# Global attention of a diffusion layer: the context scores join the latent scores' row, with one maximum and one exponential a head

## The chip, the cores and the metric

The kernel runs on one core of a Trainium2 chip. The time is device microseconds of one execution, and the median of three executions is compared. One further execution was profiled, and its trace is what the views below read. PE is the matrix engine, PEld its weight loads, DVE the vector engine, ACT the scalar engine, POOL the general engine, SP the queue from which most transfers are issued. Every engine takes its instructions in the order of its own queue.

## What is computed

A layer over 1024 latent tokens and 256 context tokens of width 1024: two attention branches side by side, gated and merged, a layer norm, and a gated feed-forward part with a short convolution. All of it is float32. The change touches the second branch, global attention with 8 heads of 64 in two groups of four, whose keys are the 1024 latent and the 256 context ones in one softmax:

```python
def _global_attention(q, k_all, v_all):
    bsz, n_tok = q.shape[:2]
    def one_block(i):
        q_blk = lax.dynamic_slice_in_dim(q, i * BLOCK, BLOCK, axis=1)
        p = jax.nn.softmax(_gqa_scores(q_blk, k_all), axis=-1)
        return _gqa_values(p, v_all)
...
    o_b = _global_attention(q_b, jnp.concatenate([k_b, k_b_c], axis=1), jnp.concatenate([v_b, v_b_c], axis=1))
```

## The kernel before

A float32 product is made of float32r ("rounded") parts: an operand is split into a high part, which is a cast, and a low part, which is what the cast left, and two or three matmuls are added up.

Attention works through 32 **units**, one for each branch, block of 128 queries and group of four heads: 16 units of the windowed branch 0, then 16 of the global branch 1, in the order (block, group). A unit of branch 1 is named 1_i_g. It has two halves:

- *Scores*, in the loop's turn u of the unit. For each head h, `lat` (L508) multiplies the queries with 1024 latent keys (four matmuls of 512 columns) into a PSUM tile `s` of two banks, of which there are two. One DVE instruction (L538) multiplies the scores by the negative scale into the SBUF tile `p` and reduces them to the head's minimum `nm` (which is minus the maximum); its second scalar is the start value of that reduction. ACT then takes the exponential in place (L505, called through `soft`) and adds up the row (`sm`).
- *Values* (`value_steps`, L601), one turn later, spread between the next unit's score steps. For each of ten blocks n of 128 keys (0 to 7 latent, 8 and 9 context), PE transposes the four heads' pieces of `p` into a PSUM tile `ptr` (L614), ACT casts it to `pth` (L623), DVE takes the rest as `ptl` (L624), and two matmuls with `pth` and `ptl` add to `av` (L635, L636). For blocks 2 and 6 ACT copies the tile out to `prw` (L620), which frees it, and POOL makes both parts.

The context keys of a unit go their own way in branch 1. `cxp` (L541), ahead of the four heads, writes the scores of all four heads with 256 context keys into a fifth `s` tile. DVE reduces it to four maxima (L550) and scales them (L551, `nmc`); ACT takes four exponentials of 256 (L505, tile `p_x`) relative to the context's maximum. `nmc` is also the start value of the latent reduction, so `nm` is the joint one. `norm` (L558) afterwards works out f = exp(nm − nmc) and POOL multiplies the context's sums and its four pieces of `p_x` by f (L564, L565, L568).

PSUM has eight banks: two `s` tiles of two, three tiles `pt` of one (transposes `ptr`, the query transposes `qtr`, the row of sums `str`, and the output tiles `b` of the first branch's projection, which fills turns 18 to 30), and one for `av`. `p` has eight SBUF tiles of 1024 columns. A unit of branch 1 takes five of them, and a tile comes free with its last transposition.

The order on each queue is not the order of the code: in this stage a list scheduler places the instructions of all turns by its own estimates, and a tile of a pool is handed on when the last reader of its previous content is done. The order it made is shown below where the prediction needs it.

Of the kernel before, what the change touches and what calls it, by code (L numbers as in the profile page):

```python
# [7 lines left out]
F32 = mybir.dt.float32  # L8
R32 = mybir.dt.float32r
AF = mybir.ActivationFunctionType  # L10
# [3 lines left out]
P = 128  # L14
D = 1024
T = 1024
# [11 lines left out]
HALF = 512  # L28
POOL_LO = (3,), (2, 6)
# [39 lines left out]
def layer_kernel(  # L69
# [393 lines left out]
    class Unit:  # L463
# [40 lines left out]
        def soft(self, s, p, h, nm, sm, scale):  # L504
            nc.scalar.activation(p, s, AF.Exp, bias=nm[:, h:h + 1], scale=scale, accum_out=sm[:, h:h + 1])  # L505

        def lat(self, h):
# [29 lines left out]
            p = p_tile(f"p{self.id}_{h}")[:, 0:T if self.br else self.w + NC]  # L537
            nc.vector.tensor_scalar(out=p, in0=o, scalar1=self.qscale(nqs)[:, hs] if self.br else -1.0,  # L538
                                    scalar2=self.other[:, hs], op0=ALU.mult, op1=ALU.min, accum_out=self.nm[:, hs])
            self.soft(p, p, h, self.nm, self.sm, -1.0)  # L540
            self.pc[h, 0] = p  # L541

        def cxp(self):
            kh = self.br * 2 + self.g
            s = s_tile(f"s{self.id}_x")
            for h in range(4):
                self.qk(s[:, h * NC:(h + 1) * NC], h, KC[0][:, kh])
            self.other = small(f"nmc_{self.id}", (P, 4))
            self.smc = small(f"smc_{self.id}", (P, 4))
            nc.vector.reduce_max(self.other, s.rearrange("p (a b) -> p a b", a=4), axis=AX.X)  # L550
            nc.vector.tensor_tensor(out=self.other, in0=self.other, in1=self.qscale(nqs), op=ALU.mult)  # L551
            p = p_tile(f"p{self.id}_x")
            for h in range(4):
                self.pc[h, 1] = p[:, h * NC:(h + 1) * NC]
                self.soft(s[:, h * NC:(h + 1) * NC], self.pc[h, 1], h, self.other, self.smc,
                          self.qscale(pqs)[:, h:h + 1])

        def norm(self):  # L558
            hc = slice(self.g * 4, self.g * 4 + 4)
            f = small(f"f_{self.id}", (P, 4))  # L560
            if self.br:
                nc.vector.tensor_tensor(out=f, in0=self.nm, in1=self.other, op=ALU.subtract)
                nc.scalar.activation(f, f, AF.Exp)
                nc.gpsimd.tensor_tensor(out=self.smc, in0=self.smc, in1=f, op=ALU.mult)  # L564
                nc.gpsimd.tensor_tensor(out=self.sm, in0=self.sm, in1=self.smc, op=ALU.add)  # L565
                for h in range(4):
                    p = self.pc[h, 1]
                    nc.gpsimd.tensor_scalar(out=p, in0=p, scalar1=f[:, h:h + 1], scalar2=0.0, op0=ALU.mult, op1=ALU.add)  # L568
            else:
                nc.vector.tensor_tensor(out=f, in0=self.nm, in1=sinkb[:, hc], op=ALU.add)  # L570
                nc.scalar.activation(f, f, AF.Exp)
                nc.vector.tensor_tensor(out=self.sm, in0=self.sm, in1=f, op=ALU.add)
                nc.vector.reciprocal(self.sm, self.sm)
# [17 lines left out]
        def score_steps(self):  # L591
            steps = [lambda h=h: self.lat(h) for h in range(4)]
            return steps + [self.norm]

        def context(self):
            self.begin()
            if self.br:
                self.cxp()

        def pslice(self, h, n):  # L600
            if self.br and n >= NT:  # L601
                return self.pc[h, 1][:, (n - NT) * P:(n - NT + 1) * P]
            return self.pc[h, 0][:, n * P:(n + 1) * P]
# [300 lines left out]
    def p_tile(name):  # L904
        return att.tile([P, T], F32, tag="p", name=name, bufs=8)
# [1019 lines left out]
```

## Time and profile before

| what | value |
|---|---|
| median of three runs | 1564.17 us (1563.13 to 1565.62) |
| profiled execution, its own time | 1565.22 us |
| span in its trace, first to last instruction | 1563.4 us |
| PE busy | 1531.6 us of the span |
| DVE, ACT, POOL busy | 1187.6, 808.6, 782.2 us |
| scores of branch 1 | from 457.9 us (first context scores) to about 744 us |
| last values of branch 1 | about 756 us |

A row of a timeline gives the start in us from the span's start, the time until the last of its instructions ends, engine, line, operation, tiles (written <- read), shape and count; in brackets stands the idle time of the engine before it and who ended that. Matmuls overlap: a row's time is a latency, and the pace of PE is read from one start to the next. Rows of groups give count, busy time, the mean of one in ns, and the idle time before them by releaser. Rows of waits give who waited for whom, the sum, the number of times and the longest.

### The profile page before, as it was taken

What the parts mean: (1) busy time and instruction counts of PE and PEld (TensorE: products, weight loads), DVE (VectorE), ACT (ScalarE), POOL (GpSimd) and SP (SyncE); (2) the same over time, 40 slices, a digit from 0 to 9 for tenths busy, and PEclk for the clock granted to TensorE, in tenths of its full rate; (3) what the DMA queues carried; (4) which work ended last, traced back from release to release, by engine and by line L of the source; (5) the groups of instructions that cost most, each with busy time, mean ns of one, the idle gap of its engine ahead of it and who ended that gap; (6) DMA issues with size and microseconds to landing.
All of it is one profiled execution on the core that took longest, in us unless ns stands there. A gap on an engine that the chain in (4) does not pass through costs nothing.

```text
span 1563.4 us, 22286 instructions
## 1 busy us (share of the span) xinstructions
PE 1531.6 (98%) x7804; PEld 1282.2 (82%) x7804; DVE 1187.6 (76%) x1714; ACT 808.6 (52%) x1431; POOL 782.2 (50%) x795
## 2 busy tenths in 40 slices
PE   9999999999999999999999999999999999999997
PEld 7888888888877877877888997888888888888887
DVE  6677976548887777777774788888888888657884
ACT  5322223358887777777431673544444444435552
POOL 0356422526666777776332455666677764121121
PEclk9999999999999999999999999999999999999998
DMA  9776662322235666631550223233334446996721
GB/s 371 267 239 239 207 245 92 106 84 66 65 116 137 150 149 151 148 80 35 180 184 16 98 79 120 81 112 115 120 102 114 113 117 191 363 265 212 251 103 55
DMA packets 113105, 232.11 MB, mean 148 GB/s; under 512 B 13056, under 2 KB 27904, under 8 KB 112896
## 3 DMA queue, kind: packets, MB, share of 16 engines
q1 hardware_dynamic: 97760, 201.82, 38.4%
q0 software_dynamic: 10400, 20.19, 8.3%
q10 hardware_dynamic: 4832, 8.68, 1.5%
q8 instruction: 61, 1.00, 0.3%
q14 instruction: 52, 0.43, 0.1%
HBM read 179.45 MB, written 65.86 MB: 157 GB/s over the span
## 4 chain that ended last, share of the span: by engine, by line
PE 54%; DVE 3%; ACT 1%; issue 1%; POOL 0%; DVEq 0%; ACTq 0%
PE p L89 4%; PE p L90 4%; PE p L91 4%; PE b L89 2%; PE b L91 2%; PE b L90 2%; PE c L89 2%; PE c L91 2%; PE d L91 2%; PE d L89 2%; PE c L90 2%; PE d L90 2%; PE a L91 2%; PE a L89 2%; PE a L90 2%; PE y L91 2%
## 5 line engine op out<-in xcount | busy, mean ns | idle before, releaser
L624 DVE TENSOR_TENSOR ptl<-ptr,pth 128x512 fp32r<-128x512 f32 x190 | 126.2, 682 | 32.6 <-ACT pth L623 32.2
L623 ACT CAST pth<-ptr 128x512 fp32r<-128x512 f32 x190 | 108.0, 593 | 54.0 <-PE ptr L614 32.6
L86 DVE TENSOR_TENSOR ld<-rd,hd 128x1024 fp32r<-128x1024 f32 x77 | 94.9, 1249 | 50.2 <-ACT hd L81 48.1
L505 ACT ACTIVATE p<-p,nm 128x1024 f32<-128x1024 f32 (+2 forms) x128 | 125.9, 985 | 4.5 <-DVE p L538 4.3
L614 PE MATMUL ptr<-ident,p 128*128 128x128 f32 x816 | 122.4, 277 | 4.4 <-DVE ptl L624 3.2
L81 ACT CAST hd<-rd 128x1024 fp32r<-128x1024 f32 x77 | 79.5, 1050 | 81.1 <-PE p L91 55.1
L614 PEld LDWEIGHTS ptr<-ident,p 128*128 128x128 f32 x816 | 94.1, 141 | 25.6 <-DVE ptl L624 7.9
L86 POOL TENSOR_TENSOR wlg<-wg,whg 128x512 fp32r<-128x512 f32 x32 | 47.7, 1500 | 123.3 <-ACT whg L81 123.3
L635 PE MATMUL av<-pth,VT 128*128 128x512 f32 x236 | 104.6, 443 | 2.1 <-ACT avs L641 1.5
L89 PE MATMUL p<-hd 128*128 128x512 f32 x264 | 103.2, 391 | 0.0
L91 PE MATMUL p<-hd,ld 128*128 128x512 f32 x264 | 102.7, 389 | 0.0
L90 PE MATMUL p<-ld,hd 128*128 128x512 f32 x264 | 102.7, 389 | 0.0
L636 PE MATMUL av<-ptl,VT 128*128 128x512 f32 x236 | 98.1, 416 | 2.7 <-POOL ptl L86 2.7
L89 PE MATMUL g<-hh,whg 128*128 128x512 f32 x256 | 99.9, 390 | 0.0
L91 PE MATMUL g<-hh,wlg 128*128 128x512 f32 x256 | 99.7, 389 | 0.0
L90 PE MATMUL g<-hl,whg 128*128 128x512 f32 x256 | 99.6, 389 | 0.0
L538 DVE TENSOR_SCALAR_CACHE_REDUCE p<-s,cvt,nmc 128x1024 f32<-128x1024 f32 x64 | 83.2, 1316 | 8.8 <-PE s L494 7.7
L493 PE MATMUL s<-KL,q 128*128 128x512 f32 (+2 forms) x192 | 75.6, 394 | 5.3 <-ACT p_x L505 2.8
L787 ACT ACTIVATE sg<-g,bgc 128x512 f32<-128x512 f32 x32 | 22.0, 686 | 96.1 <-PE g L91 96.1
L494 PE MATMUL s<-KL,q 128*128 128x512 f32 (+2 forms) x192 | 71.6, 373 | 0.0
L81 ACT CAST wS<-s 128x512 fp32r<-128x512 f32 x76 | 45.3, 620 | 46.4 <-POOL s L1227 45.7
L81 ACT CAST wA<-ru 128x512 fp32r<-128x512 f32 x57 | 35.5, 623 | 62.4 <-PE d L91 33.8
(436 smaller groups left out, 5015.2 us busy)
## 6 DMA issues: line engine op xcount, KB each, us to landing
wml<-in_wmodT_dram SPq DMA_DIRECT2D x48, 512.0 KB
ru<-in_w_up_dram SPq DMA_DIRECT2D x38, 512.0 KB
rd<-td SPq DMA_DIRECT2D x55, 256.0 KB
rd<-sd SPq DMA_DIRECT2D x44, 256.0 KB
rd<-in_w_dn_dram SPq DMA_DIRECT2D x33, 256.0 KB
wm<-in_wmodT_dram SPq DMA_DIRECT2D x16, 512.0 KB
wg<-in_w_g_dram SPq DMA_DIRECT2D x32, 256.0 KB
sgd<-sg ACTq DMA_DIRECT2D x32, 256.0 KB
```

Source lines behind the costliest of these rows:

```text
L81: nc.scalar.copy(hi, src)
L86: lo_eng.tensor_tensor(out=lo, in0=src, in1=hi.bitcast(F32), op=ALU.subtract)
L89: nc.tensor.matmul(ps, a[0], b[0], start=start, stop=False, skip_group_check=resumed)
L90: nc.tensor.matmul(ps, a[0], b[1], start=False, stop=False, skip_group_check=resumed)
L91: nc.tensor.matmul(ps, a[1], b[0], start=False, stop=stop, skip_group_check=resumed)
L505: nc.scalar.activation(p, s, AF.Exp, bias=nm[:, h:h + 1], scale=scale, accum_out=sm[:, h:h + 1])
L538: nc.vector.tensor_scalar(out=p, in0=o, scalar1=self.qscale(nqs)[:, hs] if self.br else -1.0, scalar2=self.other[:, hs], op0=ALU.mult, op1 ...
L614: nc.tensor.transpose(tr[:, h * P:(h + 1) * P], self.pslice(h, n), ident)
L623: nc.scalar.copy(hi, tr)
L624: nc.vector.tensor_tensor(out=lo, in0=tr, in1=hi.bitcast(F32), op=ALU.subtract)
L635: nc.tensor.matmul(self.av, v, hi, start=first, stop=False)
L636: nc.tensor.matmul(self.av, v, lo, start=False, stop=self.left == 0)
```

## The change

For branch 1, `p` becomes a row of 1280 columns, 1024 latent and 256 context keys. `cxp(h0)` now serves two heads: it takes a one-bank `pt` tile (`sx`), writes two times 256 context scores, takes the two heads' `p` tiles, and lets DVE scale each head's context scores into columns 1024 to 1279, with their minimum as `nmc` (new line 555; the reduction starts at the constant FBIG). It is called for heads 0 and 1 ahead of the unit's scores and for heads 2 and 3 between `lat(1)` and `lat(2)`. `lat` then writes the other 1024 columns into the same tile, and one exponential of 1280 columns with one row sum follows (new line 544). The fifth `s` tile, the reductions L550 and L551, the four exponentials of 256, `norm` in branch 1 and POOL's four multiplications go. `p` has six tiles of 1280 columns. In the windowed branch two heads share one such tile.

```diff
-            p = p_tile(f"p{self.id}_{h}")[:, 0:T if self.br else self.w + NC]
-            nc.vector.tensor_scalar(out=p, in0=o, scalar1=self.qscale(nqs)[:, hs] if self.br else -1.0,
+            if self.br:
+                p = self.pc[h]
+                row, out = p, p[:, 0:T]
+            else:
+                if h % 2 == 0:
+                    self.pair = p_tile(f"p{self.id}_{h}").rearrange("p (a b) -> p a b", a=2)
+                out = row = self.pair[:, h % 2, 0:self.w + NC]
+            nc.vector.tensor_scalar(out=out, in0=o, scalar1=self.qscale(nqs)[:, hs] if self.br else -1.0,
                                     scalar2=self.other[:, hs], op0=ALU.mult, op1=ALU.min, accum_out=self.nm[:, hs])
-            self.soft(p, p, h, self.nm, self.sm, -1.0)
+            nc.scalar.activation(row, row, AF.Exp, bias=self.nm[:, hs], scale=-1.0, accum_out=self.sm[:, hs])
...
-        def cxp(self):
+        def cxp(self, h0):
             kh = self.br * 2 + self.g
-            s = s_tile(f"s{self.id}_x")
-            for h in range(4):
-                self.qk(s[:, h * NC:(h + 1) * NC], h, KC[0][:, kh])
...
-            nc.vector.reduce_max(self.other, s.rearrange("p (a b) -> p a b", a=4), axis=AX.X)
-            nc.vector.tensor_tensor(out=self.other, in0=self.other, in1=self.qscale(nqs), op=ALU.mult)
-            p = p_tile(f"p{self.id}_x")
-            for h in range(4):
-                self.pc[h, 1] = p[:, h * NC:(h + 1) * NC]
-                self.soft(s[:, h * NC:(h + 1) * NC], self.pc[h, 1], h, self.other, self.smc,
-                          self.qscale(pqs)[:, h:h + 1])
+            s = pt_tile(f"sx{self.id}_{h0}")
+            for n, h in enumerate((h0, h0 + 1)):
+                self.qk(s[:, n * NC:(n + 1) * NC], h, KC[0][:, kh])
+            for n, h in enumerate((h0, h0 + 1)):
+                hs = slice(h, h + 1)
+                self.pc[h] = p = p_tile(f"p{self.id}_{h}")
+                nc.vector.tensor_scalar(out=p[:, T:NK], in0=s[:, n * NC:(n + 1) * NC], scalar1=self.qscale(nqs)[:, hs],
+                                        scalar2=FBIG, op0=ALU.mult, op1=ALU.min, accum_out=self.other[:, hs])
...
-            if self.br:
-                nc.vector.tensor_tensor(out=f, in0=self.nm, in1=self.other, op=ALU.subtract)
-                nc.scalar.activation(f, f, AF.Exp)
-                nc.gpsimd.tensor_tensor(out=self.smc, in0=self.smc, in1=f, op=ALU.mult)
-                nc.gpsimd.tensor_tensor(out=self.sm, in0=self.sm, in1=self.smc, op=ALU.add)
-                for h in range(4):
-                    p = self.pc[h, 1]
-                    nc.gpsimd.tensor_scalar(out=p, in0=p, scalar1=f[:, h:h + 1], scalar2=0.0, op0=ALU.mult, op1=ALU.add)
...
             steps = [lambda h=h: self.lat(h) for h in range(4)]
-            return steps + [self.norm]
+            if not self.br:
+                return steps + [self.norm]
+            steps.insert(2, lambda: self.cxp(2))
+            return steps
...
-        return att.tile([P, T], F32, tag="p", name=name, bufs=8)
+        return att.tile([P, NK], F32, tag="p", name=name, bufs=6)
```

The scheduler places the rest anew. Two places of one turn are shown; the turns of the other units of branch 1 look alike. The names: `p1_3_0_2` is the row of unit 1_3_0, head 2; `ptl1_2_1_7` the low part of block 7 of the unit before it; `bT` a product of the projection that fills in; the brackets give the engines that an instruction waits for.

First DVE's queue in the turn of unit 1_3_0, before the change, from the reciprocal of the previous unit's sums:

```order
L581 RECIPROCAL rb1_2_1_6469<-str1_2_1_6467 4x128 [waits DMAHW2_49,DMAHW7_49,DMAHW1_49,PE_49]
L538 TENSOR_SCALAR p1_3_0_2_6456,nm_1_3_0_6320<-s1_3_0_2_6451,cvt_69,nmc_1_3_0_6331 128x1024 [waits PE_49]
L538 TENSOR_SCALAR p1_3_0_3_6464,nm_1_3_0_6320<-s1_3_0_3_6459,cvt_69,nmc_1_3_0_6331 128x1024 [waits PE_49]
L624 TENSOR_TENSOR ptl1_2_1_7_6501<-ptr1_2_1_7_6495,pth1_2_1_7_6500 128x512 [waits PE_49,Activation_49]
L562 TENSOR_TENSOR f_1_3_0_6475<-nm_1_3_0_6320,nmc_1_3_0_6331 128x4 [waits DVE_49]
L951 TENSOR_TENSOR bT0_5_6510<-b0_5_0_6512,bT0_5_6510 128x512 [waits DMAHW6_49,PE_49]
L624 TENSOR_TENSOR ptl1_2_1_8_6545<-ptr1_2_1_8_6539,pth1_2_1_8_6544 128x512 [waits Activation_49]
L624 TENSOR_TENSOR ptl1_2_1_9_6554<-ptr1_2_1_9_6548,pth1_2_1_9_6553 128x512 [waits PE_49,Activation_49]
```

The same place in DVE's queue after the change:

```order
L572 RECIPROCAL rb1_2_1_6355<-str1_2_1_6353 4x128 [waits DMAHW2_49,DMAHW7_49,DMAHW1_49,PE_49]
L617 TENSOR_TENSOR ptl1_2_1_7_6385<-ptr1_2_1_7_6379,pth1_2_1_7_6384 128x512 [waits PE_49,Activation_49]
L944 TENSOR_TENSOR bT0_5_6394<-b0_5_0_6396,bT0_5_6394 128x512 [waits DMAHW6_49,PE_49]
L555 TENSOR_SCALAR p1_3_0_2_6342,nmc_1_3_0_6218<-sx1_3_0_2_6337,cvt_69 128x256 [waits PE_49]
L555 TENSOR_SCALAR p1_3_0_3_6344,nmc_1_3_0_6218<-sx1_3_0_2_6337,cvt_69 128x256 [waits PE_49]
L542 TENSOR_SCALAR p1_3_0_2_6342,nm_1_3_0_6216<-s1_3_0_2_6346,cvt_69,nmc_1_3_0_6218 128x1024 [waits DVE_49]
L542 TENSOR_SCALAR p1_3_0_3_6344,nm_1_3_0_6216<-s1_3_0_3_6361,cvt_69,nmc_1_3_0_6218 128x1024 [waits DVE_49]
L617 TENSOR_TENSOR ptl1_2_1_8_6429<-ptr1_2_1_8_6423,pth1_2_1_8_6428 128x512 [waits Activation_49]
L617 TENSOR_TENSOR ptl1_2_1_9_6438<-ptr1_2_1_9_6432,pth1_2_1_9_6437 128x512 [waits Activation_49]
```

The two instructions of 1024 columns for heads 2 and 3 moved from ahead of `ptl` 7 to behind it, with two of 256 columns in front of them, each of which waits for PE.

Then PE's queue at the turn from unit 1_3_0 to 1_3_1, before the change, right behind the last transposes of block 9 (`s1_3_1_x` is the tile of context scores, `q11`, `q21` the two query tiles):

```order
L636 MATMUL av1_2_1_6404<-ptl1_2_1_5_6446,VT2_2137 128x512
L493 MATMUL s1_3_1_x_6561<-KC_2134,q11_3_1_6289 128x256
L494 MATMUL s1_3_1_x_6561<-KC_2134,q21_3_1_6290 128x256 [waits DMAHW5_49,DMAHW4_49]
L493 MATMUL s1_3_1_x_6561<-KC_2134,q11_3_1_6289 128x256
L494 MATMUL s1_3_1_x_6561<-KC_2134,q21_3_1_6290 128x256
```

And after it, four `av` matmuls and the two heads' context scores `sx1_3_1_0` behind those transposes:

```order
L494 MATMUL s1_3_1_0_6479<-KL3_2133,q11_3_1_6185 128x512 [waits DVE_49]
L495 MATMUL s1_3_1_0_6479<-KL3_2133,q21_3_1_6186 128x512
L494 MATMUL s1_3_1_0_6479<-KL3_2133,q11_3_1_6185 128x512
L495 MATMUL s1_3_1_0_6479<-KL3_2133,q21_3_1_6186 128x512
L494 MATMUL s1_3_1_1_6527<-KL3_2133,q11_3_1_6185 128x512 [waits DVE_49]
L495 MATMUL s1_3_1_1_6527<-KL3_2133,q21_3_1_6186 128x512
L494 MATMUL s1_3_1_1_6527<-KL3_2133,q11_3_1_6185 128x512
L607 MATMUL ptr1_3_0_0_6455<-ident_58,p1_3_0_0_6224 128x128 [waits DVE_49,PE_49]
L607 MATMUL ptr1_3_0_0_6455<-ident_58,p1_3_0_1_6226 128x128
L607 MATMUL ptr1_3_0_0_6455<-ident_58,p1_3_0_2_6342 128x128 [waits Activation_49]
L629 MATMUL av1_2_1_6291<-ptl1_2_1_8_6429,VT4_2139 128x512
L628 MATMUL av1_2_1_6291<-pth1_2_1_9_6437,VT4_2139 128x512
```

The latent scores of the next unit's heads 0 and 1 moved from behind the first two blocks of transposes to ahead of them, and each now waits for DVE.

A little later in the same queue, after the change:

```order
L607 MATMUL ptr1_3_0_2_6486<-ident_58,p1_3_0_0_6224 128x128 [waits DVE_49]
L607 MATMUL ptr1_3_0_2_6486<-ident_58,p1_3_0_1_6226 128x128
L607 MATMUL ptr1_3_0_2_6486<-ident_58,p1_3_0_2_6342 128x128
L607 MATMUL ptr1_3_0_2_6486<-ident_58,p1_3_0_3_6344 128x128
L495 MATMUL s1_3_1_1_6527<-KL3_2133,q21_3_1_6186 128x512
L607 MATMUL ptr1_3_0_3_6497<-ident_58,p1_3_0_0_6224 128x128 [waits Activation_49]
```

The first transpose of block 3 waits for ACT; before the change it waited for DVE (the same line then read [waits DVE_49]).

More of the change, by code (lines that the diff above doesn't have):

```diff
@@ L28 @@
 HALF = 512
+FBIG = 3.0e38
 POOL_LO = (3,), (2, 6)
@@ L502, in qscale @@
             return t[:, self.i, self.g * 4:self.g * 4 + 4]
-        def soft(self, s, p, h, nm, sm, scale):
-            nc.scalar.activation(p, s, AF.Exp, bias=nm[:, h:h + 1], scale=scale, accum_out=sm[:, h:h + 1])
         def lat(self, h):
@@ L560, in norm @@
             f = small(f"f_{self.id}", (P, 4))
[L561 to L573 removed]
+            nc.vector.tensor_tensor(out=f, in0=self.nm, in1=sinkb[:, hc], op=ALU.add)
+            nc.scalar.activation(f, f, AF.Exp)
+            nc.vector.tensor_tensor(out=self.sm, in0=self.sm, in1=f, op=ALU.add)
+            nc.vector.reciprocal(self.sm, self.sm)
         def rows(self):
@@ L597, in context @@
             if self.br:
-                self.cxp()
+                self.other = small(f"nmc_{self.id}", (P, 4))
+                self.cxp(0)
         def pslice(self, h, n):
-            if self.br and n >= NT:
-                return self.pc[h, 1][:, (n - NT) * P:(n - NT + 1) * P]
-            return self.pc[h, 0][:, n * P:(n + 1) * P]
+            return self.pc[h][:, n * P:(n + 1) * P]
         def value_steps(self):
```

4 lines of the change are left out of this document (1 added, 3 removed).

## Prediction

> **What bounds the kernel now.** I read the page, the busy time by stage, the waits of PE and its weight loads in the stage of the second branch, and then that stage's timelines. The page's span, and the stage in three windows (PE, PEld, DVE, ACT, POOL busy, then the clock):
>
> ```profile
> span 1563.4 us, 22286 instructions
> PE 54%; DVE 3%; ACT 1%; issue 1%; POOL 0%; DVEq 0%; ACTq 0%
> 458.00:500.00 42.00, 36.68 (x203) 28.68 (x204) 32.45 (x55) 33.45 (x79) 27.59 (x43) 0.96 0.60 142
> 500.00:755.00 255.00, 248.65 (x1438) 204.37 (x1438) 194.76 (x297) 186.47 (x401) 190.59 (x275) 1.00 0.48 116
> 755.00:1563.00 808.00, 796.32 (x3851) 671.97 (x3849) 627.16 (x670) 372.55 (x506) 363.37 (x243) 0.99 0.46 144
> ```
>
> PE sets the end, in this stage and behind it: from 500 to 755 us it is idle for only 255 − 248.65 = 6.4 us. ACT (73%), POOL (75%) and DVE (76%) have room. What leaves those three is worth something only where PE waits for it, and 755 to 1563 us is PE work too, so a shift at 755 should reach the end whole. Who kept PE and its weight loads waiting:
>
> ```profile
> PEld av L635 <- ACT avs L641: 5.7, 11, 0.7
> PEld s L493 <- ACT p_x L505: 5.3, 6, 1.0
> PEld av L636 <- POOL ptl L86: 1.0, 2, 0.7
> PEld s L493 <- DVE p L538: 0.5, 1, 0.5
> PEld av L636 <- POOL ptl L86: 2.8, 2, 1.8
> ```
>
> The first four are of 500 to 755 us, the last of 458 to 500. Six times the next scores wait until ACT has read the four context scores out of the `s` tile. What one costs, and PE's pace, is read from start to start:
>
> ```profile
> 671.91 0.60 PE L614 MATMUL ptr<-ident,p_x 128*128 128x128 f32 x4
> 672.27 0.48 PE L636 MATMUL av<-ptl,VT 128*128 128x512 f32 x1
> 672.59 0.28 PE L493 MATMUL s_x<-KC,q 128*128 128x256 f32 x1
> 672.71 0.28 PE L494 MATMUL s_x<-KC,q 128*128 128x256 f32 x1
> ...
> 677.91 0.40 PE L636 MATMUL av<-ptl,VT 128*128 128x512 f32 x1
> 678.90 0.50 PE L493 MATMUL s<-KL,q 128*128 128x512 f32 x1 [0.59 <-ACT p_x L505]
> 679.24 0.39 PE L494 MATMUL s<-KL,q 128*128 128x512 f32 x1
> 679.47 0.40 PE L493 MATMUL s<-KL,q 128*128 128x512 f32 x1
> ```
>
> A block of four transposes takes 0.36, the first matmul of 512 behind it 0.32, further ones 0.23, one of 256 columns 0.12. The wait at 677.91 costs 0.99 − 0.23 = 0.76, not the 0.59 of its idle time. By the same rule (each start-to-start step of the 203 and 1438 PE records less the usual step of its kind) I count 9.0 us lost from 458 to 500 and 13.3 from 500 to 755: 22.3 in all. That is the most that any relief here can win.
>
> **The change, part by part.** The groups of DVE, ACT and POOL that go or stretch:
>
> ```profile
> L538 DVE TENSOR_SCALAR_CACHE_REDUCE p<-s,cvt,nmc 128x1024 f32<-128x1024 f32 x64 | 83.2, 1316 | 8.8 <-PE s L494 7.7 <-PE ptr L614 0.5
> L538 DVE TENSOR_SCALAR_CACHE_REDUCE p<-s,negsink 128x640 f32<-128x640 f32 x48 | 41.3, 875 | 1.5 <-PE s L494 1.4
> L538 DVE TENSOR_SCALAR_CACHE_REDUCE p<-s,negsink 128x512 f32<-128x512 f32 x16 | 11.4, 742 | 0.4 <-PE s L494 0.4
> L550 DVE TENSOR_REDUCE nmc<-s_x 128x4 f32<-128x1024 f32 x16 | 19.5, 1217 | 2.2 <-PE s_x L494 2.2
> L551 DVE TENSOR_TENSOR nmc<-nmc,cvt 128x4 f32<-128x4 f32 x16 | 10.2, 636 | 0.2
> L505 ACT ACTIVATE p<-p,nm 128x1024 f32<-128x1024 f32 x64 | 74.6, 1166 | 2.1 <-DVE p L538 1.8
> L505 ACT ACTIVATE p<-p,nm 128x640 f32<-128x640 f32 x48 | 39.9, 834 | 2.0 <-DVE p L538 2.0
> L505 ACT ACTIVATE p_x<-s_x,nmc,cvt 128x256 f32<-128x256 f32 x64 | 35.3, 565 | 6.7 <-DVE nmc L551 6.7
> L568 POOL TENSOR_SCALAR p_x<-p_x,f 128x256 f32<-128x256 f32 x64 | 29.8, 477 | 0.0
> L620 ACT COPY prw<-ptr 128x512 f32<-128x512 f32 x46 | 27.2, 590 | 23.0 <-PE ptr L614 20.3 <-POOL ot L650 2.3 <-POOL p_x L568 0.4
> ```
>
> *Work.* POOL loses 4 × 0.48 = 1.9 us a unit. ACT loses four exponentials of 256, 4 × 0.57 = 2.3, and each of the other four grows by 256 columns at (1166 − 834) / 384 = 0.86 ns, to 1.39 us: 0.9 in all. DVE loses 1.22 + 0.64 and gains four instructions of 256. No such row stands there. From 512 and 640 the slope is 1.04 ns a column, 742 − 266 = 476 ns; from 640 and 1024 it is 1.15 ns and 434. I take 0.45, near both; the instruction of 512, 0.74, is the upper end. DVE comes out even. PE's matmuls stay the same in number and shape, but the new order alternates more often between transposes and the other matmuls, 156 times against 129, and each costs 0.32 − 0.23 = 0.09: +2.4 us. None of the work is on the path by itself; what it releases is. The paired rows of the windowed branch add no wait to DVE's or ACT's queue there, and cost nothing as long as PE covers them.
>
> [...]
>
> *What goes.* The `s` waits for `p_x`, and with them most of what else PE lost from 500 to 755: I let 11.8 of those 13.3 go and keep 1.5 (POOL, single places). From 458 to 500 I keep 6.3 of 9.0: those are POOL's, which there stands behind a transfer, and the slower clock after it (below), 1.6 + 0.8 + 2.1 + 1.8.
>
> *What comes.* `p` has six tiles, and a unit now holds four until block 9 is transposed, since the context's columns lie in the same rows. Heads 0 and 1 of the next unit take the other two. So heads 2 and 3 cannot be written before block 9 of the previous unit is through; before, with a tile of its own for the context, block 7 was enough. The order shows it: DVE's four instructions for heads 2 and 3 moved behind `ptl` 7, and the first two wait for PE. Behind block 9 PE has little left that doesn't need them. The paces:
>
> ```profile
> 560.39 1.33 DVE L538 TENSOR_SCALAR_CACHE_REDUCE p<-s,cvt,nmc 128x1024 f32<-128x1024 f32 x1
> 561.66 0.07 DVE L538 DVE_READ_ACCUMULATOR p<-s,cvt,nmc 128x1 f32 x1
> 561.66 0.67 DVE L624 TENSOR_TENSOR ptl<-ptr,pth 128x512 fp32r<-128x512 f32 x1
> ```
>
> ```profile
> 476.62 1.34 DVE L538 TENSOR_SCALAR_CACHE_REDUCE p<-s,cvt,nmc 128x1024 f32<-128x1024 f32 x1 [0.23 <-PE s L494]
> ```
>
> ```profile
> 478.02 0.50 PE L493 MATMUL s<-KL,q 128*128 128x512 f32 x1 [0.53 <-DVE p L538]
> ```
>
> ```profile
> 577.25 1.16 ACT L505 ACTIVATE p<-p,nm 128x1024 f32<-128x1024 f32 x1
> ...
> 578.51 1.15 ACT L505 ACTIVATE p<-p,nm 128x1024 f32<-128x1024 f32 x1
> ```
>
> ```profile
> L614 PE MATMUL ptr<-ident,p 128*128 128x128 f32 x532 | 74.5, 275 | 4.0 <-DVE ptl L624 3.2 <-ACT q L486 0.6
> ```
>
> DVE goes on 1.27 after an instruction of 1024 (0.06 less than its length; so 0.39 to 0.41 after one of 256), ACT 1.26 after an exponential of 1024 (so 1.48 after one of 1280), PE follows DVE after 0.06 (477.96 to 478.02), and a transpose lasts 0.27. With t = 0 at the start of block 9's transposes:
>
> DVE: head 2's context at 0.36, head 3's at 0.77, head 2's 1024 from 1.2 to 2.56, head 3's from 2.5 to 3.83. ACT: exponential 2 from 2.7, 3 from 4.17 until 5.65, its accumulator read included.
> PE: transposes 0.36, four `av` 1.02, four `sx` 0.47: 1.85. The next unit's first scores need an `s` tile, free at 2.62: **0.77** lost. They end at 3.55; the second `s` tile is free at 3.89: **0.34** lost. Three matmuls 0.70, three transposes 0.24, two `av` 0.55: 5.38; the fourth transpose needs exponential 3, 5.71: **0.33** lost. Five transposes 0.46, `av` 0.32, block 2 0.36, one matmul 0.32: 7.17. Block 3 waits for the tile that ACT copies out as `prw`: block 2 ends at 7.1, the copy takes 0.59 and ends at 7.75, PE goes on at 7.81: **0.64** lost.
>
> That is 2.08 a turn. What DVE and ACT have ahead of these (`ptl` 7, `bT`, the cast of the queries) is done by t = 0, 3 us after block 7. Queued behind the waiting instructions are `ptl` 8 and 9 and the next unit's context, done by 5.85, which PE needs at 6.5; the `sx` tile, which holds one of three `pt` places from mid-turn, is free at 1.3. Nine turns have this order; four have one `av` more ahead of the first score, 1.85; one has three more, 1.4; and the last, which has no next unit's scores to put between, loses 2.0 at the exponential of head 2 and 0.5 at that of head 3. The sum is 18.7 + 7.4 + 1.4 + 2.5 = 30.0. At 0.74 for the 256-column instruction it is 9 us more; without the wait for `prw`, which hangs on ACT's casts of blocks 0 and 1 coming first, 9 less.
>
> **The sum.** 30.0 + 2.4 + 1.5 + 6.3 = 40.2 against 22.3 before: +17.9. The profiled execution took 1565.22 with a span of 1563.4 and lies 1.05 above the median; the same difference on the median of 1564.17 gives **1582**.
>
> **The rivals.** *Faster:* if those waits are covered, only the relief is left: 10.2 against 22.3, −12, 1552. For it the chain behind block 9 would have to be 1.4 us shorter, more than a whole instruction of 1024 columns, and ACT's copy early as well. PE's waits for `p_x` and the chain's shares for DVE and ACT speak for it; the `s` tiles against it, since they are free only when the rows are written. 0.11.
>
> *Half of it:* only the two waits for `s` (1.1 a turn, 16.7 over 15) come, because the exponential is hidden by the first two and ACT's copy is early: 26.9 against 22.3, +4.6, 1569. 0.17.
>
> *No difference* beyond 0.2% (3.1 us, about what a measurement of this kernel tells from none): the shallow case with a lucky start of the stage. 0.05. That the change doesn't do what it says is excluded by the order, in which `p_x`'s instructions are gone.
>
> *The clock:*
>
> ```profile
> 480.00:500.00 20.00, 17.27 (x93) 13.20 (x92) 13.39 (x22) 13.36 (x30) 12.51 (x20) 0.91 0.38 75
> 484.77 1.64 PE L614 MATMUL ptr<-ident,p 128*128 128x128 f32 x8 [1.80 <-DVE ptl L624]
> ```
>
> After an idle time of 1.80 us the granted clock was 0.91 over 20 us, 1.8 us lost. If every turn's waits did that, 14 × 1.8 = 25 us would come on top: 1607. Its single waits are shorter, 0.3 to 0.8. 0.06. [...]
>
> **How the numbers follow.** The forecast keeps 0.61 and is the likeliest. Slower by over 0.2%: 0.61 + 0.17 + 0.06 = 0.84; within: 0.05; faster: 0.11. The range leaves out the faster rival and the clock, 0.17: from 1564 (the shallow case at its shortest) to 1592 (the sum with the 0.74 of DVE's upper end, somewhat less since not all turns are in step).
>
> **What would show it.** After: idle time on DVE before line 555, ended by PE's `ptr`, once a turn; PE before the latent scores waiting for DVE's line 542, some 14 times 0.5 to 0.8 and 14 times about 0.3; PE's `ptr` waiting for `prw`; no wait for `p_x`. The stage from the first context scores to the last values takes some 18 us longer and nothing behind it changes. It would be wrong if DVE doesn't wait for PE there, if PE's idle time in the stage falls, or if the stage is longer and the end isn't.

## The result, and the profile after

The changed kernel takes 1573.26 us (median of six, 1572.80 to 1574.99) against 1564.43 for the kernel before on the same chip: 1.0060 of its time, with an interval of 1.0047 to 1.0073. That is 8.8 us slower. The forecast was 1582 in a range of 1564 to 1592: the direction was right, and the change costs half of what was forecast. The profiled execution took 1573.05. Its span, its chain by engine and its three windows (columns as before):

```profile
span 1570.9 us, 22111 instructions
PE 88%; DVE 7%; ACT 2%; issue 1%; POOL 1%; DMA 0%; SPq 0%; DVEq 0%; ACTq 0%; POOLq 0%
458.00:500.00 42.00, 39.81 (x231) 31.23 (x231) 35.49 (x73) 32.54 (x60) 28.54 (x38) 1.00 0.65 168
500.00:762.00 262.00, 248.16 (x1395) 196.47 (x1394) 185.52 (x358) 164.84 (x273) 154.85 (x184) 0.99 0.46 109
762.00:1570.00 808.00, 797.90 (x3871) 673.54 (x3869) 627.51 (x673) 374.66 (x509) 370.27 (x245) 0.99 0.46 144
```

ACT and POOL have less to do, as the change intends (over the whole span ACT is busy for 787.8 us instead of 808.6, POOL for 754.3 instead of 782.2), and PE idles 262 − 248.2 = 13.8 us in the stage where it idled 6.4. Who kept its weight loads waiting from 458 to 766 us, and DVE's wait ahead of line 555:

```profile
PEld s L494 <- DVE p L542: 16.1, 29, 0.7
PEld ptr L607 <- ACT prw L613: 10.6, 15, 0.8
PEld ptr L607 <- ACT p L544: 5.9, 17, 2.2
```

```profile
DVE p L555 <- PE ptr L607: 12.6, 15, 0.9
```

These are the signs that the prediction named: DVE waits once a turn for block 9, PE waits twice a turn for an `s` tile and once for the `prw` copy, and no wait for `p_x` is left. The third row's waits of the weight loads make PE's own steps late almost only in the last turn (1.97 us at 754.45). One turn, PE first:

```profile
544.94 0.28 PE L495 MATMUL sx<-KC,q 128*128 128x256 f32 x1
545.75 0.50 PE L494 MATMUL s<-KL,q 128*128 128x512 f32 x1 [0.53 <-DVE p L542]
...
546.55 0.39 PE L495 MATMUL s<-KL,q 128*128 128x512 f32 x1
547.02 0.50 PE L494 MATMUL s<-KL,q 128*128 128x512 f32 x1
...
548.62 0.73 PE L607 MATMUL ptr<-ident,p 128*128 128x128 f32 x5
...
549.78 0.48 PE L495 MATMUL s<-KL,q 128*128 128x512 f32 x1
550.70 0.66 PE L607 MATMUL ptr<-ident,p 128*128 128x128 f32 x4 [0.44 <-ACT prw L613]
```

From start to start, less the usual step, the three waits cost 0.81 − 0.12 = 0.69, 0.47 − 0.23 = 0.24 and 0.92 − 0.32 = 0.60. The second shows no bracket at all: PE's rows overlap, and only the distance of the starts gives it away. The same turn on DVE and on ACT:

```profile
543.53 0.49 DVE L555 TENSOR_SCALAR_CACHE_REDUCE p<-sx,cvt 128x256 f32<-128x256 f32 x1 [0.92 <-PE ptr L607]
...
544.35 1.34 DVE L542 TENSOR_SCALAR_CACHE_REDUCE p<-s,cvt,nmc 128x1024 f32<-128x1024 f32 x1
545.61 0.08 DVE L542 DVE_READ_ACCUMULATOR p<-s,cvt,nmc 128x1 f32 x1
```

```profile
545.73 1.37 ACT L544 ACTIVATE p<-p,nm 128x1280 f32<-128x1280 f32 x1 [1.24 <-DVE p L542]
...
547.09 1.35 ACT L544 ACTIVATE p<-p,nm 128x1280 f32<-128x1280 f32 x1
548.35 0.18 ACT L544 ACTIVATION_READ_ACCUMULATOR p<-p,nm 128x1 f32 x1
```

The last value matmul of the stage started at 756.11 us before and starts at 766.21 now, 10.1 later, while the span grew by 7.5: some 2.6 came back behind the stage. Of that 1.7 is the clock. In five microseconds with a granted clock of 0.66 (the column third from the end) it is 0.50 for 3.41 us, from 850.72 in the kernel before and from 755.54 in the changed one, an estimated loss of 3.41 × 0.5 = 1.7: matmuls of 512 columns start 0.43 apart from 851.05 to 854.04, where the usual step is 0.23. Here are such windows, first of the kernel before, then of the changed one:

```profile
850.00:855.00 5.00, 5.00 (x16) 3.92 (x15) 1.69 (x5) 0.00 (x0) 1.03 (x1) 0.66 0.01 3
```

```profile
755.00:760.00 5.00, 4.88 (x24) 4.00 (x25) 2.56 (x5) 3.38 (x7) 1.15 (x2) 0.66 0.06 17
857.00:862.00 5.00, 4.83 (x30) 3.98 (x29) 1.91 (x6) 0.00 (x0) 1.65 (x2) 1.00 0.00 0
```

```profile
754.45 0.99 PE L607 MATMUL ptr<-ident,p 128*128 128x128 f32 x4 [1.81 <-ACT p L544]
```

Before, the clock fell once behind the stage (and once at its start, at 485 us); now it falls in the stage's last turn, after the idle time of 1.81 us in the last row, and stays at 1.00 at the place where it was 0.50 before. (It is 0.50 in both once more, from 1553.86 and from 1561.09 us on, where PE has no matmul left.) The remaining 0.9 of the 2.6 I can't assign.

### The profile page after: what moved, and what is told of

Its sections match the earlier page's. It is cut to its first block, busy times and chain, and to the rows that moved or that the text cites. A ratio compares the mean times of both kernels' runs of the same rounds, so it can differ in the third digit from the quotient of the medians.

```text
span 1570.9 us, 22111 instructions
## 1 busy us (share of the span) xinstructions
PE 1535.7 (98%) x7804; PEld 1278.4 (81%) x7804; DVE 1181.4 (75%) x1794; ACT 787.8 (50%) x1287; POOL 754.3 (48%) x699
## 4 chain that ended last, share of the span: by engine, by line
PE 88%; DVE 7%; ACT 2%; issue 1%; POOL 1%; DMA 0%; SPq 0%; DVEq 0%; ACTq 0%; POOLq 0%
PE ptr L607 6%; PE p L90 4%; PE p L92 4%; PE p L91 4%; PE g L90 4%; PE g L91 4%; PE g L92 4%; PE b L92 3%; PE b L90 3%; DVE p L542 3%; PE b L91 3%; PE av L628 3%; PE av L629 3%; PE s L494 2%; PE c L90 2%; PE c L91 2%
## 5 line engine op out<-in xcount | busy, mean ns | idle before, releaser
L607 PE MATMUL ptr<-ident,p 128*128 128x128 f32 x944 | 144.6, 278 | 8.8 <-ACT prw L613 6.0
L544 ACT ACTIVATE p<-p,nm 128x1280 f32<-128x1280 f32 (+2 forms) x128 | 139.0, 1088 | 20.5 <-DVE p L542 20.4
L607 PEld LDWEIGHTS ptr<-ident,p 128*128 128x128 f32 x944 | 109.4, 141 | 41.7 <-ACT prw L613 10.9
L628 PE MATMUL av<-pth,VT 128*128 128x512 f32 x236 | 101.4, 430 | 0.7 <-ACT avs L634 0.4
L494 PE MATMUL s<-KL,q 128*128 128x512 f32 (+2 forms) x192 | 79.5, 414 | 9.1 <-DVE p L542 7.9
L495 PE MATMUL s<-KL,q 128*128 128x512 f32 (+2 forms) x192 | 73.0, 380 | 0.0
```

What stands on the lines that cost most here:

```text
L494: nc.tensor.matmul(o, self.q[0][:, hs], ks, start=True, stop=False)
L544: nc.scalar.activation(row, row, AF.Exp, bias=self.nm[:, hs], scale=-1.0, accum_out=self.sm[:, hs])
L607: nc.tensor.transpose(tr[:, h * P:(h + 1) * P], self.pslice(h, n), ident)
L628: nc.tensor.matmul(self.av, v, hi, start=first, stop=False)
```

## The experiments

The losses below are made as in the prediction: PE's steps from start to start, each less the usual step of its kind, added up from the first context scores to the last value matmul and grouped by the tile that the late matmul writes. "Scores" are `s` and `sx` together, "values" are `av`. Each ratio is to the kernel before timed together with that run on the same chip (1563.1 to 1564.4 us), so that the first two columns don't divide exactly. What PE loses inside the stage while the granted clock is 0.50 is counted as lost too.

| kernel | time, us | ratio to the kernel before | lost | scores | transposes | values |
|---|---|---|---|---|---|---|
| before | 1564.4 | 1 | 22.3 | 6.5 | 7.1 | 7.9 |
| changed | 1573.3 | 1.0060 (1.0047 to 1.0073) | 31.7 | 15.2 | 15.1 | 1.4 |
| changed, seven rows | 1571.4 | 1.0048 (1.0035 to 1.0060) | 25.5 | 8.7 | 10.3 | 5.9 |
| its control, six rows | 1576.8 | 1.0085 (1.0070 to 1.0101) | 34.0 | 15.5 | 16.0 | 2.5 |
| changed, POOL's blocks 0 and 6 | 1569.9 | 1.0045 (1.0031 to 1.0059) | 27.1 | 16.9 | 4.9 | 5.3 |
| both of these | 1564.6 | 1.0007 (0.9998 to 1.0016) | 21.1 | 5.0 | 9.9 | 5.7 |
| both, and `avs` by DVE | 1561.4 | 0.9991 (0.9982 to 1.0000) | 18.7 | 3.2 | 10.4 | 4.6 |
| before, context scores in `pt` places | 1568.2 | 1.0031 (1.0021 to 1.0041) | 24.5 | 4.2 | 12.8 | 7.1 |
| before, without POOL's scaling | 1559.0 | 0.9970 (0.9959 to 0.9981) | 17.7 | 3.9 | 5.9 | 7.6 |
| changed, context scores in `s` tiles | 1558.8 | 0.9971 (0.9959 to 0.9984) | 16.8 | 6.8 | 8.1 | 1.9 |
| changed, first pair in an `s` tile | 1579.0 | 1.0099 (1.0085 to 1.0112) | 36.1 | 22.8 | 8.3 | 3.2 |
| changed, later scores | 1569.5 | 1.0036 (1.0022 to 1.0050) | 26.8 | 4.9 | 15.7 | 2.4 |
| changed, later scores and blocks 0 and 6 | 1563.0 | 0.9999 (0.9990 to 1.0008) | 22.4 | 6.7 | 10.1 | 5.0 |
| seven rows, blocks, `avs`, `s` tiles | 1559.4 | 0.9969 (0.9957 to 0.9981) | 16.7 | 6.4 | 7.4 | 2.8 |

My theory at the start was the prediction's: six rows make heads 2 and 3 wait for block 9. The rivals were that the four short DVE instructions and the place that `sx` takes make the loss, and that one queue stands behind everything.

### Seven rows, and the control for it

```diff
-        return att.tile([P, NK], F32, tag="p", name=name, bufs=6)
+        return att.tile([P, NK], F32, tag="p", name=name, bufs=7)
...
-            r = wpool.tile([P, 8, P], F32, tag="wraw", name=f"rwb{br}_{key}", bufs=1)
+            r = ht(f"rwb{br}_{key}", (P, 8, P))
+            hput(f"rwb{br}_{key}")
```

> The changed kernel with seven p tiles instead of six; to make room, the staging tile of the projection weights lies in a free slot of the big pool instead of the attention pool. Theory (rows): the waits of latent scores for DVE's line 542 come from heads 2 and 3 having no row until block 9 of the previous unit is transposed. With seven, only head 3 has none. In 458 to 766 us the weight loads' and PE's waits for `s` (16.1 + 6.1 us idle in the changed kernel) fall below 6, PE's losses from 31.8 to 15 to 21, the time from 1573 to 1556 to 1563. The waits for `prw` (16.6) stay. Rival (small instructions): the four DVE instructions of 256 columns and the transposes' place held by `sx` make the waits; then the `s` waits stay within 3 us of 22 and the time at 1572 to 1575.

The control has the last two lines without the seventh row.

> The changed kernel with six p tiles as it is, and only the staging tile of the projection weights moved to a free slot of the big pool: the control for the run with seven. Both theories: 1572 to 1576, the waits for `s` and `prw` as in the changed kernel. If it is faster than 1570, the place of that tile and not the seventh row has to be counted in the run with seven.

The control is 3.5 us slower than the changed kernel, 0.8 above what both theories gave. ACT's first cast of those weights moves from 697.8 to 741.8 us, and the stage loses 2.3 more, about 0.9 of it in the last turn; what makes the rest stays open. So the seventh row has to be compared with 1576.8, and takes 5.4 off that. The control's wait for `s`, then PEld's waits in the kernel with seven:

```profile
PEld s L494 <- DVE p L542: 16.2, 29, 0.7
```


```profile
PEld ptr L607 <- ACT prw L613: 7.9, 17, 0.8
PEld s L494 <- DVE p L542: 6.7, 18, 0.5
PEld ptr L607 <- DVE ptl L617: 5.2, 9, 1.7
PEld av L628 <- ACT avs L634: 5.2, 16, 0.5
PEld av L628 <- ACT pth L616: 3.5, 9, 0.8
```

The wait for `s` falls from 16.2 in the control to 6.7, so the rows do make the greater part of it. But only part of it comes out at the end: 3.4 us more are now lost ahead of the value matmuls, which wait for ACT's casts and its copy of `av`. The theory had the mechanism, not the size: its time was 1556 to 1563.

### POOL's blocks, and both together

```diff
-POOL_LO = (3,), (2, 6)
+POOL_LO = (3,), (0, 6)
```

> The changed kernel with POOL's two blocks of the second branch 0 and 6 instead of 2 and 6, so that the first place that comes free behind a turn's start hangs on an ACT copy of block 0 and on no DVE subtraction. Theory: block 3 waits 0.58 us in each turn because two of three `pt` places wait for DVE's subtractions, which stand behind head 0's row, and the third for ACT's copy of block 2. With block 0 copied first, the waits for `prw` fall from 16.6 us to under 4 and the time from 1573 to 1563 to 1567. Rival: the place is scarce whichever block is copied, since `sx` takes one of the three for a part of the turn; a wait for `ptl` or `prw` of the same size comes at another block, and the time stays at 1571 to 1576.

The 10.6 us of waits for `prw` are gone; in their place the values wait for ACT, as with seven rows:

```profile
PEld s L494 <- DVE p L542: 15.8, 28, 1.0
PEld ptr L607 <- ACT p L544: 6.1, 16, 2.3
PEld av L628 <- ACT avs L634: 3.4, 14, 0.2
PEld av L628 <- ACT pth L616: 3.3, 6, 1.0
```

So 10.2 go ahead of the transposes, 3.9 come ahead of the values and 1.7 ahead of the scores. The time is 2.9 above the theory's and just below the rival's: the wait goes, and more than half of what it gives comes back elsewhere. Both together:

> The changed kernel with both: seven p tiles (staging tile in a slot of the big pool) and POOL's blocks 0 and 6. From start to start PE lost in the stage 31.7 us in the changed kernel, of it 14.5 ahead of latent scores and 15.1 ahead of transposes; seven rows left 7.1 and 10.3, the blocks 15.8 and 4.9, and in both 4 to 4.5 more appeared ahead of the values' matmuls. Theory (two separate waits): both go, 7 + 5 + about 6 = 18 are left with some at other tiles, the time is 1560 to 1565. Rival (one queue behind all of them: ACT, whose exponential of 1280 takes 1.37): what one wait frees the next takes, the values' matmuls wait for ACT's casts and copies by 10 or more, 24 or more are lost, 1567 to 1571.

The time is at the theory's upper end, 1564.6, with 21.1 lost: the two waits are separate, and values wait no longer than with one of them alone. It is no faster than the kernel before.

> The run with seven rows and POOL's blocks 0 and 6, and besides the copy of a unit's finished values out of the `av` bank (0.6 us, one a unit) made by DVE instead of ACT. Theory (ACT's queue): the values of the next unit wait for that copy behind an exponential of 1.37; on DVE it comes earlier in most turns, 3 to 5 us less than without this step. Rival: DVE's row instruction of 1.34 us stands ahead of it as the exponential did on ACT, and the time stays within 2 us or is worse.

```diff
-                nc.scalar.copy(avs, av)
+                (nc.vector.tensor_copy if self.br else nc.scalar.copy)(avs, av)
```

The time falls by 3.2, which the theory gave; but where it falls fits only in part, since 1.1 go ahead of values and 1.8 ahead of scores, which wait for ACT too little to explain it. What ties the scores to that copy stays open.

### The parts of the change, put into the kernel before

> The kernel before with one part of the change alone: its context scores go by head pairs into two transposes' places instead of an `s` tile, with maximum, exponentials, POOL's scaling and eight p tiles as before. Theory: the waits of latent scores for `p_x` (5.3 us idle, 6 times about 0.76 from start to start) go and nothing comes in their place: 1564.4 becomes 1558 to 1562. Rival (small instructions and places): two places held at the start of each unit keep the transposes waiting, 14 turns by 0.3 to 0.6, and the four short DVE instructions stand before the subtractions: 1566 to 1572.

```diff
-            s = s_tile(f"s{self.id}_x")
-            for h in range(4):
-                self.qk(s[:, h * NC:(h + 1) * NC], h, KC[0][:, kh])
...
+            for h0 in (0, 2):
+                s = pt_tile(f"sx{self.id}_{h0}")
+                for n in (0, 1):
+                    self.qk(s[:, n * NC:(n + 1) * NC], h0 + n, KC[0][:, kh])
...
```

The rival holds by its time, though not by its shape, fourteen turns of 0.3 to 0.6. The scores' loss falls from 6.5 to 4.2, and the transposes' rises from 7.1 to 12.8. In three turns a transpose is late by about 1.4, as here, where it waits for DVE's subtraction to free its place (lines 617 and 627 of this kernel):

```profile
587.00 0.33 PE L617 MATMUL ptr<-ident,p 128*128 128x128 f32 x1 [1.20 <-DVE ptl L627]
```

A transposes' place is thus not free for the context scores even where the rows are plenty. Some 1.7 us of the loss may be clock: in this trace it falls twice at the start of the stage (478 and 488 us, behind waits of 1.8; 0.80 to 0.85 in the four windows of 5 us from 475 to 495), once in the kernel before (0.66 from 485 to 490).

> The kernel before without POOL's four multiplications of the context exponentials per unit (L568): that scaling is left out of the result, all else is as before. It asks what POOL's relief is worth by itself. Theory: the 9.0 us that PE lost from 458 to 500 us come mostly from POOL standing behind a transfer with 1.9 us of multiplications a unit still to do; without them that loss is 3 to 6, the rest of the stage loses 1 less (the two waits of values for POOL's `ptl`), and the time is 1558 to 1561. Rival (POOL has room, the start waits for the transfer and for DVE): the loss from 458 to 500 stays at 8 to 9.5 and the time at 1563 to 1565.

```diff
-                for h in range(4):
-                    p = self.pc[h, 1]
-                    nc.gpsimd.tensor_scalar(out=p, in0=p, scalar1=f[:, h:h + 1], scalar2=0.0, op0=ALU.mult, op1=ALU.add)
```

The time falls as the theory said, by 4.1, but not where it said. Over 458 to 500 us alone about 9 are still lost (9.0 before). The gain comes from later, most of it ahead of scores and transposes. PEld's waits for `p_x` and for POOL's `ptl` over the whole stage, 5.9 and 3.8 in the kernel before, are now:

```profile
PEld s L493 <- ACT p_x L505: 3.0, 5, 1.0
...
PEld av L633 <- POOL ptl L86: 2.6, 3, 1.8
```

So POOL's relief is real, and the loss at the start of the stage does not hang on it.

### The place, undone

```diff
-            s = pt_tile(f"sx{self.id}_{h0}")
+            s = s_tile(f"sx{self.id}_{h0}")
```

> The changed kernel with one part undone: the context scores of a head pair lie in an `s` tile and not in a transposes' place; all else as in the changed kernel, six rows. Theory (places): the 15.1 us lost ahead of transposes come from `sx` holding one of three places; they fall below 8, and the two `s` tiles, now used six times a unit and not four, cost 5 to 15 more than 14.5 ahead of scores: 1570 to 1582. Rival (rows and queues): the transposes' losses stay at 13 or more, since they hang on the order of DVE's and ACT's queues, and the `s` losses come on top: 1578 to 1590.

The theory of places has the transposes right (8.1 of 15.1), and both failed on the scores: their loss halves as well, though the two `s` tiles are used six times a unit instead of four. At 1558.8 it is faster than the kernel before. In a turn of it, DVE first, then PE behind block 9 (transposes at 539.46):

```profile
539.78 0.48 DVE L555 TENSOR_SCALAR_CACHE_REDUCE p<-sx,cvt 128x256 f32<-128x256 f32 x1 [0.42 <-PE ptr L607]
...
541.96 1.34 DVE L542 TENSOR_SCALAR_CACHE_REDUCE p<-s,cvt,nmc 128x1024 f32<-128x1024 f32 x1
```

```profile
540.84 0.40 PE L494 MATMUL s<-KL,q 128*128 128x512 f32 x1
541.08 0.39 PE L495 MATMUL s<-KL,q 128*128 128x512 f32 x1
541.30 0.39 PE L494 MATMUL s<-KL,q 128*128 128x512 f32 x1
541.53 0.39 PE L495 MATMUL s<-KL,q 128*128 128x512 f32 x1
...
542.56 0.28 PE L495 MATMUL sx<-KC,q 128*128 128x256 f32 x1
...
543.37 0.50 PE L494 MATMUL s<-KL,q 128*128 128x512 f32 x1 [0.31 <-DVE p L542]
```

From 483 us on DVE's order is word for word that of the changed kernel (ahead of it a few instructions of the first turns change places), the rows are still six, and DVE still waits for block 9. What differs is what PE has to do meanwhile. In the changed kernel the scores of heads 2 and 3 stand in both `s` tiles before block 6, and behind block 9 PE has four value matmuls and four context scores left, 1.85 − 0.36 = 1.5 us, for a chain of 2.2. Here the second pair's context scores take one of the two tiles, so head 3's four score matmuls (540.84 to 541.75, 0.93 us) fall behind block 9, just into the gap.

### The gap filled in another way

That reading makes a forecast of its own: with the rows and the places as they are, more work for PE behind block 9 takes the wait away.

```diff
-SPAN = 0.8, 0.85
+SPAN = 0.8, 1.05
```

> The changed kernel with its context scores in a transposes' place and six rows as they are, and one number changed: the score steps of a second-branch unit are spread over 1.05 of the turn instead of 0.85. DVE's order stays word for word; on PE the four transposes of the next queries and three of the value matmuls come behind block 9 instead of ahead of block 8. Theory (PE has nothing left in the gap): block 9 to the first free `s` tile takes the same time, but PE has 0.36 + 3 by 0.23 = 1.05 us more to do in it; the loss ahead of scores falls from 14.5 to 3 to 7, the loss ahead of transposes stays at 13 to 16, and the time falls from 1573 to 1563 to 1567. Rival (the rows themselves): DVE is that much later as well, the loss ahead of scores stays above 12 and the time at 1571 to 1575.

```profile
PEld ptr L607 <- ACT prw L613: 9.2, 14, 0.8
PEld sx L494 <- ACT q L487: 5.2, 12, 0.8
...
PEld s L494 <- DVE p L542: 1.9, 7, 0.4
```

```profile
749.84 0.79 PE L90 MATMUL b<-O,hwb 128*128 128x512 f32 x1 [1.75 <-POOL O L84]
```

The loss ahead of `s` falls to 1.3 (4.9 with the context scores, which now wait for the queries), the wait for `prw` stays, and DVE's wait for block 9 is still there with 9.0 us. (In this run DVE's order differs at 484 us and from 711 us on.) So late rows cost PE next to nothing as long as it has other work. The time came out 2.5 above the forecast: the last turn, which is moved as well, has 5.7 of losses instead of 3.2, the row at 749.84 among them, and between 750 and 755 us the granted clock is 0.50.

> The changed kernel with its first pair of context scores (heads 0 and 1) in an `s` tile and the second pair in a transposes' place as in the changed kernel; DVE's order and six rows as before it. Both pairs in `s` tiles took the loss ahead of transposes from 15.1 to 8.1 and ahead of scores from 14.5 to 6.7. Theory (two costs of the place): the first pair's place is what block 3 lacks at the start of a turn, so the loss ahead of transposes falls to 7 to 10; the scores of heads 2 and 3 still stand in both `s` tiles ahead of block 6, so the loss ahead of scores stays at 11 to 16; 1564 to 1569. Rival (one cost): both fall or both stay; 1557 to 1561 or 1572 to 1576.

```diff
-            s = pt_tile(f"sx{self.id}_{h0}")
+            s = (pt_tile if h0 else s_tile)(f"sx{self.id}_{h0}")
```

One half of the theory holds: the first pair's place is worth 6.8 of the 15.1 ahead of transposes. The other half failed, and with it the time, 10 above the forecast. The scores of heads 2 and 3 stand in both tiles as before, and now the next unit's context scores, too, need a tile that the late rows hold:

```profile
548.15 0.39 PE L494 MATMUL sx<-KC,q 128*128 128x256 f32 x1 [0.78 <-DVE p L542]
549.42 0.50 PE L494 MATMUL s<-KL,q 128*128 128x512 f32 x1 [0.53 <-DVE p L542]
```

I had counted what the pair no longer takes and not what it takes instead: of the 1.5 us of work in the gap, 0.47 was the context scores.

### Order alone, and all of it

```diff
-POOL_LO = (3,), (2, 6)
+POOL_LO = (3,), (0, 6)
...
-        for lst, of, sp in ((ss, 0.0, SPAN[u >= 17]), (vs, VOFF, VSPAN), (fs, 0.0, 1.0)):
+        for lst, of, sp in ((ss, 0.0, 1.05 if 17 <= u < 31 else SPAN[u >= 17]), (vs, VOFF, VSPAN), (fs, 0.0, 1.0)):
```

> The changed kernel with its places and six rows as they are, and only the order changed: score steps spread over 1.05 of the turn up to the last but one unit of the second branch (the last turn as in the changed kernel), and POOL's blocks 0 and 6. The later scores alone took the loss ahead of scores from 14.5 to 1.3 (with 2.9 more ahead of the context scores), and lost about 5 in the last turn; the blocks alone took 10.2 off the loss ahead of transposes and put 3.9 on that ahead of values. Theory (the change lost time by what PE and ACT had next to do, not by its rows or places as such): both gains hold together and the last turn's loss goes, 15 to 19 us are lost of 31.7, the time is 1556 to 1561, below the kernel before. Rival (with places and rows so few, what leaves one wait comes back in another): 24 or more, 1565 to 1570.

```profile
PEld s L494 <- DVE p L542: 2.7, 8, 0.5
...
PEld ptr L607 <- ACT prw L613: 1.2, 3, 0.4
```

Both regular waits are gone together, and the changed kernel is level with the one before: the order, and the choice of the blocks that POOL makes, take the whole loss back with rows and places as the change has them. Neither number was met; 22.4 are lost, in between. What is left of the transposes' losses is some 50 small ones, 0.11 on average, and 4.6 in the last turn, where the granted clock is 0.50 from 745.6 to 752.4 us. The clock weighs on this kernel's time: four executions with a mean granted clock of 0.998 took 1561.5 to 1561.8, three with 0.993 took 1564.9 to 1565.4.

> The changed kernel with both pairs of context scores in `s` tiles, seven p tiles (staging tile in a slot of the big pool), POOL's blocks 0 and 6, and the copy out of the `av` bank on DVE. With the pairs in `s` tiles alone 16.8 us were lost in the stage and the time was 1558.8; with the other three alone 18.7 and 1561.4. Theory (separate waits): what each takes away is partly the same, 12 to 15 us are left, the time is 1553 to 1558. Rival (a floor of single places and the last turn, about 17): 1558 to 1561.

The rival: 16.7 lost and 1559.4, no better than the `s` tiles alone. These two are the fastest versions here that compute the whole layer, each 0.3% faster than the kernel before. A part of such a gain can be clock. With the context scores in `s` tiles the mean granted clock of the executions is 0.9967 against 0.9957 in the kernel before; at 0.996 in both, the times are 1559.6 and 1562.7, 3.1 of the 4.2 us between the medians.

## Why the prediction was right in kind and twice too large

**What held.** Step by step: DVE's wait for block 9, the first `s` wait (0.69; forecast 0.77), the second (0.24; 0.34), the wait for `prw` (0.60; 0.64), fourteen turns of them, the last turn (3.2; 2.5), and the end of the waits for `p_x`. POOL's other block took away the wait that it was to take, the seventh row more than half of its own.

**The terms that were off.** From the first context scores before (457.9) to the last values, the sum was 30.0 + 2.4 + 1.5 + 6.3 = 40.2 against 22.3. Measured:

- *The turns, 30.0:* 8.2 (first `s`) + 3.4 (second) + 8.3 (`prw`) + 3.2 (last turn) = 23.1. The largest gap is the wait for head 3's exponential, 0.33 a turn, which never came except in the last turn. With block 9's transposes at 543.22 as t = 0, that exponential starts at 3.87 and its accumulator is read by 5.31, where I had 4.17 and 5.65, and PE comes to the transpose at 5.40. The start was 0.19 earlier for the first exponential, and ACT goes on 1.36 after an exponential of 1280, not 1.48: I had added 0.09 to the length, as with 1024 columns, where the rows now show 0.01 less than the length.
- *Switches, 2.4:* by this count the work itself, without losses, grew by 0.5 (276.4 to 276.9) for 29 more switches. The term failed because I priced one side of a switch. The first matmul behind transposes takes 0.32 instead of 0.23; but the last transpose ahead of a matmul takes a step of 0.03 instead of 0.11. A block of four and a matmul, 0.36 + 0.32, costs what five plain steps do, 4 × 0.11 + 0.23.
- *The start, kept at 6.3:* 2.0. POOL's wait behind the transfer (1.9 us from 458 to 500, now 0.3) and the slower clock at 485 us (0.96 from 458 to 500, now 1.00) both went. POOL's multiplications alone were not the reason: the kernel without them loses as much there. Which other part of the change did it, no run here separates.
- *The rest of the stage, kept at 1.5:* 6.8, in single losses that are nearly all under 0.12. Some 1.2 of it are clock: it is at 0.50 for 3.4 us from 755.5, and a transpose there takes a step of 0.21 instead of 0.11.
- *Behind the stage, 0:* −2.6, of it 1.7 the clock.

23.1 + 0.5 + 2.0 + 6.8 = 32.4, less 22.3 is the 10.1 by which the stage's end moved; with −2.6 that is the span's 7.5. The terms that were too high (turns 6.9, switches 1.9, start 4.3, behind the stage 2.6) add up to 15.7, and the rest of the stage, too low by 5.3, hides a third of that: to that extent it is luck that the sum is not further off.

**What the explanation lacked.** It put the waits down to the six rows. The rows are a condition, and the runs could answer it in two ways: in part by a seventh row, or, with six, by leaving PE work for the gap. The prediction listed PE's work behind block 9 correctly and treated it as given; but it was a result of the same edit, which had moved the context scores out of the `s` tiles and so let the scores of heads 2 and 3 run ahead. Undoing that one line turns +0.60% into −0.29%. With it undone, the change brings a relief of 0.3%, as much as the kernel before gains without POOL's scaling; that it is the same relief isn't shown. The place, with the order that comes with it, costs 0.9%.

**The rivals.** *Half of it* came nearest by time, and by the wrong route: it left out the `prw` wait, which is there, and let the start stay. *Faster* would have needed the chain to be hidden; the later scores show that 1.05 us of moved work is enough for the scores' part. *The clock* did not come: fourteen turns with three waits of 0.2 to 0.7 us each left it at 1.00 from 500 to 750 us, as the six waits of about 0.8 did in the kernel before.

## What to carry to other kernels

When an edit moves a result into another buffer, ask two questions: what the new buffer keeps waiting, and what the freed one lets run ahead. Work that runs ahead is missing later, in the gap that it used to fill. Here the late rows cost PE time only where it had nothing else in its queue (with the later scores DVE still waits 9.0 us for block 9, and 1.3 are lost ahead of `s`), so list the consumer's queue behind the wait, under the new order, before pricing the wait. And price a switch between two kinds of instructions on both sides of it: here 0.32 instead of 0.23 on one, 0.03 instead of 0.11 on the other.

## What the runs showed of the hardware

- The clock: in the kernel before it is 0.50 for 3.413 us from 850.72, with PE idle for only 0.17 us in the three before that, and with matmuls of one column from 847.5 to 849.7. In the changed kernel the same stretch, 10.2 us later and with the same 0.17, leaves it at 1.00 (857 to 862 us); of the fourteen traces eight show this fall (a granted clock below 1.00 between 845 and 870) and six do not. In these two kernels the falls begin whole multiples of 3.413 us apart: from 485.49 to 850.72 us in the kernel before are 107 of them, from there to 1553.86 are 206, and in the changed kernel from 755.54 to 1561.09 are 236. So 1.7 us of a difference between two kernels can be one such fall, which one of them has and the other has not; what makes it come was not shown.
- A DVE instruction of 256 columns from PSUM with a reduction, which the prediction had to estimate at 0.45 us, has a mean of 0.479; the next one starts 0.41 after it. ACT's exponential of 1280 columns takes 1.372 (estimate 1.39):

```profile
L555 DVE TENSOR_SCALAR_CACHE_REDUCE p<-sx,cvt 128x256 f32<-128x256 f32 x64 | 28.4, 479 | 12.7 <-PE ptr L607 12.6
L544 ACT ACTIVATE p<-p,nm 128x1280 f32<-128x1280 f32 x64 | 87.7, 1372 | 17.8 <-DVE p L542 17.8
```
